# Mixer B: the probabilities turned by VectorE and GpSimd instead of by TensorE

## The chip, the core and the metric

One core of a Trainium2 chip runs the whole program. The metric is the device time of one execution in microseconds (us). An engine works through its own instructions in order: TensorE (PE), VectorE (DVE), ScalarE (ACT), GpSimd (POOL) and SyncE (SP), which issues most of the DMAs. They wait for each other by semaphores.

## What is computed

An encoder of two layers over 256 tokens with 2048 features, all in float32. Layer 0 has mixer A (grouped-query attention), layer 1 has mixer B. A gated MLP follows each mixer. Mixer B is what the change touches. It has 24 heads of 128 features in three groups (windows and dilations (128,1), (512,4), (2048,16)), eight heads to a group:

```python
def dilated_group(q, k, v, rel_bias_g, window, dilation):
    ...                       # keys gathered by stride, masked to the window
    logits = einsum(qb, kb) * scale + bias
    m = max(logits); p = exp(logits - m); l = sum(p)
    o = einsum(p, vb) / l
    return o, m + log(l)      # and the log of the softmax denominator

def mixer_b(h, w_qkv, w_o, rel_bias):
    qkv = h @ w_qkv
    ...                       # outs, log_zs of the three groups
    wts = softmax(stack(log_zs), axis=0)
    y = concat([wts[g] * outs[g] for g in range(3)])
    return y @ w_o
```

The product of probabilities and values needs the probabilities with the keys on the partitions. The softmax leaves them with the queries on the partitions. So each 128x128 block of probabilities has to be turned (transposed) once. This turning is what the change is about.

## The kernel before

The work is a long row of projections. A weight matrix is streamed from HBM in pieces of 4 x 128 rows by 512 columns. `feed` handles one piece: two DMAs of 512 KB into `raw`, and for each half of the piece one "tile" of 128x1024 numbers. ACT rounds the tile to a high part `wh` (L156), VectorE subtracts to get the low part `wl` (L157), and TensorE multiplies it in 12 matmuls of 512 columns (L144, L145, L146: high by high, low by high, high by low). There are four buffers each of `raw`, `wh` and `wl`, so ACT and VectorE can be at most four tiles ahead of TensorE. The subtraction and rounding are given a priority 60 instructions ahead of their place, so that they come early in their engines' order.

All attention work is written as Python generators that are put into a list (`start`). Each half piece of a projection calls `step`, which advances the first generator by one `yield`. So the attention of one projection is interleaved, step by step, with the matmuls of the next ones. The order on every engine is fixed when the program is built.

Mixer B goes over two halves (`hf`) of four heads per group. In each half the keys and queries of the three groups are projected first; `k_gen` and `s_gen` turn them and compute the scores and the exponentials `pr`. The end of the last `s_gen` computes the combined weights `e` from all three groups' maxima and sums (L785 to L793). Then the values of groups 0, 1 and 2 are projected, and for each `v_gen(g, ...)` starts:

- before the change, one step of `v_gen` handles one head: VectorE multiplies `pr` by the weights `e` (L807), TensorE turns the result block by block into PSUM (L809, by a multiplication with the identity), and ACT and VectorE copy it to SBUF as `pT` (group 0: split in a high and a low part, L196 and L197; groups 1 and 2: one copy on ACT or VectorE in turn, L68 or L70). The next step multiplies `pT` and the values (L210 to L212 in group 0, L208 in groups 1 and 2) and splits the product into `ah` and `al`.
- group 0 has 2x2 blocks for a head, groups 1 and 2 have two: 16 + 8 + 8 blocks in a half, 64 in all.

`stg` (two buffers), `qTh`, `qTl`, `kTh`, `kTl` are names of SBUF buffers. In this stretch they have no other use: they hold the scaled projections and the turned queries and keys while `k_gen` and `s_gen` run.

VectorE has a transpose of its own, used elsewhere in the kernel (`block_T`, L237): it turns blocks of 32x32, each within its 32 partitions. To bring a block to another 32 partitions, `block_T` writes 32 partitions at a time, sixteen instructions for a tile.

Of the kernel before, what the change touches and what calls it, by code (L numbers as in the profile page):

```python
# [7 lines left out]
F32 = mybir.dt.float32  # L8
F32R = mybir.dt.float32r
AF = mybir.ActivationFunctionType  # L10
ALU = mybir.AluOpType
AX = mybir.AxisListType

P = 128
D = 2048
NT = 256
# [12 lines left out]
def tile_encoder(ctx: ExitStack, tc: tile.TileContext, x, xT, w_a, w_ao, q_gain, k_gain, w_b, w_bo,  # L29
                 rel_bias, gains, w_up, conv, w_down, final_norm, rope, ident_c, onehot, out):  # L30
    nc = tc.nc
# [10 lines left out]
    ident = cpool.tile([P, P], F32, name="ident")  # L42
# [13 lines left out]
    def nm(s):  # L56
        uid[0] += 1
        return f"{s}_{uid[0]}"

    def ps_tile():  # L60
        return psp.tile([P, 512], F32, tag="ps", name=nm("ps"))
# [3 lines left out]
    def copy(o, i):  # L65
        turn[0] ^= 1
        if turn[0]:
            nc.scalar.activation(o, i, AF.Copy)  # L68
        else:
            nc.vector.tensor_copy(o, i)  # L70
# [121 lines left out]
    def split(hi, lo, src):  # L192
        if lo is None:
            copy(hi, src)
            return
        nc.scalar.activation(hi, src, AF.Copy)  # L196
        nc.vector.tensor_tensor(lo, src, hi.bitcast(F32), ALU.subtract)  # L197
# [7 lines left out]
    def mm3(o, lhsT, rhs, ls, rs, start, stop):  # L205
        (lh, ll), (rh, rl) = lhsT, rhs
        if ll is None:
            nc.tensor.matmul(o, lh[ls], rh[rs], start=start, stop=stop)  # L208
            return
        nc.tensor.matmul(o, lh[ls], rh[rs], start=start, stop=False)  # L210
        nc.tensor.matmul(o, lh[ls], rl[rs], start=False, stop=False)  # L211
        nc.tensor.matmul(o, ll[ls], rh[rs], start=False, stop=stop)  # L212

    def pair_tile(pool, shape, tag, bufs=1, whole=False):
        if whole:
            return pool.tile(shape, F32, tag=tag + "h", name=nm(tag), bufs=bufs), None
        return tuple(pool.tile(shape, F32R, tag=tag + c, name=nm(tag + c), bufs=bufs) for c in "hl")
# [5 lines left out]
    def new_slot(kt):  # L223
        return (hpool.tile([P, NT], F32R, tag=f"ah{kt}", name=nm("ah")),
                hpool.tile([P, NT], F32R, tag=f"al{kt}", name=nm("al")))
# [254 lines left out]
    def evac_split(pool, accs, rstd, whole=False):  # L480
        hi, lo = pair_tile(pool, [P, 2, 512], "v", 1, whole)
        for m in range(2):
            split_scaled(hi[:, m, :], lo if lo is None else lo[:, m, :], accs[m], rstd[:, m:m + 1])
        return hi, lo
# [14 lines left out]
    def heads_T_dve(o, s, pool, tag):  # L499
# [7 lines left out]
        if lo is not None:  # L507
            split(hi, lo, t)

    def mixer_a():  # L510
        with tc.tile_pool(name="apool", bufs=1) as ap:
            junk = junk_of(ap)
# [110 lines left out]
            v = evac_split(ap, va, rstd[0])  # L623
# [85 lines left out]
    def mixer_b(hT, ss_in):  # L709
        with tc.tile_pool(name="bpool", bufs=1) as bp:  # L710
# [25 lines left out]
            allp = slice(None)  # L736
            for hf in range(2):
# [3 lines left out]
                probs = []  # L741
                e = small.tile([P, 3, 8], F32, tag="e", name=nm("e"))
# [49 lines left out]
                    nc.vector.reciprocal(mn, mn)  # L792
                    nc.vector.tensor_tensor(e, e, mn[:, None, :].to_broadcast([P, 3, 8]), ALU.mult)  # L793

                def v_gen(g, accs, hf=hf, probs=probs, e=e):
                    v = evac_split(bp, accs, rstd, g > 0)
                    pTs = {}
                    yield
                    for k in range(5):
                        yield  # L800
                        if k < 4:
                            i = k
                            pr = probs[4 * g + i]
                            t = ps_tile()
                            for m in range(2):
                                c = 4 * m + i
                                nc.vector.tensor_scalar(pr[m], pr[m], e[:, g, c:c + 1], None, op0=ALU.mult)  # L807
                                for kt in range(2 if g == 0 else 1):
                                    nc.tensor.transpose(t[:, kt * NT + m * P:kt * NT + (m + 1) * P],  # L809
                                                        pr[m][:, kt * P:(kt + 1) * P], ident)  # L810
                            pT = pTs[i] = pair_tile(bp, [P, 2 * NT], "pT", 2, g > 0)
                            n = 2 * NT if g == 0 else NT
                            split(pT[0][:, :n], pT[1] if pT[1] is None else pT[1][:, :n], t[:, :n])
                        if k >= 1:
                            i = k - 1
                            j = i % 2
                            pT = pTs.pop(i)
                            if j == 0:
                                o = ps_tile()
                            for kt in range(2):  # L820
                                vs = (allp, kt, slice(i * P, (i + 1) * P))
                                if g == 0:
                                    mm3(o[:, j * NT:(j + 1) * NT], v, pT, vs,
                                        (allp, slice(kt * NT, (kt + 1) * NT)), kt == 0, kt == 1)
                                else:
                                    mm3(o[:, j * NT + kt * P:j * NT + (kt + 1) * P], v, pT, vs,
                                        (allp, slice(kt * P, (kt + 1) * P)), True, True)
                            sl = (2 * g + hf) * 4 + i
                            slots[sl] = new_slot(sl)
                            hi, lo = slots[sl]  # L830
                            split(hi, lo, o[:, j * NT:(j + 1) * NT])

                for g in range(3):
                    bts = biases(hf, g)
# [6 lines left out]
                for g in range(3):  # L841
                    start(v_gen(g, project(w_b, 6 * g + 4 + hf, hT, kgs)))
            return *out_proj(w_bo, slots, [0, 2, 4, 1, 3, 5], 3, 3, junk, bp, "vl"), cw

    hT, ss, cw = mixer_a()
    hT, ss = ffn(0, hT, ss, cw, 2, False, bias_lines)
    hT, ss, cw = mixer_b(hT, ss)
# [85 lines left out]
```

## Time and profile before

| | |
|---|---|
| three runs | 2293.26, 2293.84, 2293.91 us (median 2293.84) |
| profiled execution | 2293.58 us, its span 2291.6 us |
| PE busy | 2279.6 us (99%) |
| DVE busy | 1632.4 us (71%) |
| ACT busy | 1220.7 us (53%) |
| POOL busy | 151.6 us (7%) |

The span runs from the first to the last instruction of the core; some 2 us of the execution lie outside it. Mixer B runs from about 997 to 1555 us of the span. The turning of probabilities (L809) begins at 1160.8 us in the first half and at 1374.3 us in the second.

### The profile page before, as it was taken

Reading aid. Unit: us, or ns where it says so; the run is one execution under the profiler, and the core shown is the slowest. Engines: PE = TensorE matmul, PEld = TensorE weight load, DVE = VectorE, ACT = ScalarE, POOL = GpSimd, SP = SyncE. Lnnn points to the kernel's source line nnn. Section 1 sums busy time; section 2 is a strip of 40 time slices with the busy share of each in tenths; the row PEclk is TensorE's granted clock in tenths of the full one; section 3 lists DMA queues with packets and bytes.
Section 4 is the critical chain, followed back from the end, with each engine's and each line's share of the span. In section 5 each row is a group of like instructions: output and inputs, shape, how many; then the busy total and the mean of one; then the engine's idle time right before and its main releaser. Section 6 shows DMA issues by size and latency. Waiting matters only on the chain.

```text
span 2291.6 us, 31034 instructions
## 1 busy us (share of the span) xinstructions
PE 2279.6 (99%) x11633; PEld 1945.6 (85%) x11633; DVE 1632.4 (71%) x2280; ACT 1220.7 (53%) x1746; POOL 151.6 (7%) x147
## 2 busy tenths in 40 slices
PE   9999999999999999999999999999999999999998
PEld 7888888888888888888888888888888888888886
DVE  6877877775557776878866885677777744777754
ACT  7565565554345554545454554445555533555543
POOL 2331000000000000010000000000000000000010
PEclk9999999999999999999999999999999999999999
DMA  8545655566655556576655554566555566565564
GB/s 300 166 132 162 202 191 187 188 192 190 193 193 189 190 191 191 186 217 208 188 171 181 180 189 164 176 200 204 191 187 190 187 195 194 190 191 187 192 191 149
DMA packets 257015, 433.43 MB, mean 189 GB/s; under 512 B 13784, under 2 KB 194776, under 8 KB 256736
## 3 DMA queue, kind: packets, MB, share of 16 engines
q1 hardware_dynamic: 254912, 425.64, 57.7%
q0 software_dynamic: 1520, 5.25, 1.1%
q8 instruction: 91, 1.49, 0.3%
q10 hardware_dynamic: 432, 0.56, 0.1%
q14 instruction: 60, 0.49, 0.1%
HBM read 429.20 MB, written 2.20 MB: 188 GB/s over the span
## 4 chain that ended last, share of the span: by engine, by line
PE 98%; DVE 1%; issue 1%; DMA 0%; ACT 0%; POOL 0%; SPq 0%; POOLq 0%; DVEq 0%; ACTq 0%
PE acc L123 28%; PE acc L145 17%; PE acc L146 17%; PE acc L144 17%; PE acc L121 15%; PE ps L208 1%; PE ps L211 1%; PE ps L212 0%; PE ps L210 0%; PE ps L665 0%; PE ps L809 0%; DVE wl L157 0%; DVE tT L237 0%; DMA raw<-in_w_a_dram 0%; POOL t L597 0%
## 5 line engine op out<-in xcount | busy, mean ns | idle before, releaser
L157 DVE TENSOR_TENSOR wl<-raw,wh 128x1024 fp32r<-128x1024 f32 (+1 forms) x456 | 553.7, 1217 | 319.6 <-ACT wh L156 316.0
L156 ACT ACTIVATE wh<-raw 128x1024 fp32r<-128x1024 f32 (+1 forms) x456 | 475.4, 1046 | 514.3 <-PE acc L146 443.0
L123 PE MATMUL acc<-xh,wh 128*128 128x512 f32 x2816 | 673.8, 391 | 0.0
L123 PEld LDWEIGHTS acc<-xh,wh 128*128 128x128 f32 x2816 | 517.0, 188 | 100.5 <-DVE v L356 0.4
L112 DVE TENSOR_TENSOR wl<-raw,wh 128x1024 fp32r<-128x1024 f32 x352 | 458.8, 1304 | 194.9 <-ACT wh L111 194.9
L111 ACT ACTIVATE wh<-raw 128x1024 fp32r<-128x1024 f32 x352 | 372.7, 1059 | 208.9 <-issue 77.7
L144 PE MATMUL acc<-wh,ah 128*128 128x512 f32 x1024 | 399.0, 390 | 0.0
L145 PE MATMUL acc<-wl,ah 128*128 128x512 f32 x1024 | 398.5, 389 | 0.0
L146 PE MATMUL acc<-wh,al 128*128 128x512 f32 x1024 | 398.5, 389 | 0.0
L121 PEld LDWEIGHTS acc<-xh,wl 128*128 128x128 f32 x2816 | 361.6, 191 | 14.0
L121 PE MATMUL acc<-xh,wl 128*128 128x256 f32 x2816 | 366.3, 283 | 0.0
L144 PE MATMUL acc<-wh,xh 128*128 128x512 f32 x768 | 302.6, 395 | 1.0 <-ACT wh L156 1.0
L145 PE MATMUL acc<-wl,xh 128*128 128x512 f32 x768 | 299.8, 390 | 0.2 <-DVE wl L157 0.2
L146 PE MATMUL acc<-wh,xh 128*128 128x512 f32 x768 | 299.5, 390 | 0.0
L146 PEld LDWEIGHTS acc<-wh,al 128*128 128x128 f32 x1024 | 192.2, 188 | 39.9
L144 PEld LDWEIGHTS acc<-wh,ah 128*128 128x128 f32 x1024 | 192.3, 188 | 39.6
L145 PEld LDWEIGHTS acc<-wl,ah 128*128 128x128 f32 x1024 | 192.2, 188 | 39.3
L146 PEld LDWEIGHTS acc<-wh,xh 128*128 128x128 f32 x768 | 144.2, 188 | 30.6
L144 PEld LDWEIGHTS acc<-wh,xh 128*128 128x128 f32 x768 | 144.4, 188 | 29.1 <-ACT wh L156 1.4
L145 PEld LDWEIGHTS acc<-wl,xh 128*128 128x128 f32 x768 | 144.4, 188 | 27.8 <-DVE wl L157 0.5
L375 POOL TENSOR_TENSOR cv<-cg,cv 128x512 f32<-128x512 f32 x44 | 62.0, 1408 | 1163.3 <-DVE cv L367 1163.3
L355 ACT ACTIVATE v<-acc 128x256 f32<-128x256 f32 x176 | 66.3, 377 | 113.7 <-PE acc L123 113.7
(156 smaller groups left out, 1364.1 us busy)
## 6 DMA issues: line engine op xcount, KB each, us to landing
raw<-in_w_up_dram SPq DMA_DIRECT2D x352, 512.0 KB, 4.0
raw<-in_w_down_dram SPq DMA_DIRECT2D x176, 512.0 KB, 4.2
raw<-in_w_b_dram SPq DMA_DIRECT2D x144, 512.0 KB, 3.8
raw<-in_w_bo_dram SPq DMA_DIRECT2D x48, 512.0 KB, 3.7
raw<-in_w_a_dram SPq DMA_DIRECT2D x40, 512.0 KB, 4.5
raw<-in_w_ao_dram SPq DMA_DIRECT2D x32, 512.0 KB, 3.7
raw<-in_w_a_dram SPq DMA_DIRECT2D x16, 256.0 KB, 5.8
h<-in_x_dram SPq DMA_DIRECT2D x4, 512.0 KB, 7.6
```

The costliest lines, as they stand in the source:

```text
L111: nc.scalar.activation(wh, rk, AF.Copy)
L112: nc.vector.tensor_tensor(wl, rk, wh.bitcast(F32), ALU.subtract)
L121: nc.tensor.matmul(acc[j][:, :NT], wl[:, kt, c], lhs[4 * kg + kt][0], start=st, stop=sp)
L123: nc.tensor.matmul(acc[j], wh[:, kt, c], lhs[4 * kg + kt][2], start=st, stop=sp)
L144: nc.tensor.matmul(accs[m], xh[:, c], wh[:, j, :], start=st, stop=False)
L145: nc.tensor.matmul(accs[m], xh[:, c], wl[:, j, :], start=False, stop=False)
L146: nc.tensor.matmul(accs[m], xl[:, c], wh[:, j, :], start=False, stop=sp)
L156: nc.scalar.activation(wh[:, c], r[:, c], AF.Copy)
L157: nc.vector.tensor_tensor(wl[:, c], r[:, c], wh[:, c].bitcast(F32), ALU.subtract)
L208: nc.tensor.matmul(o, lh[ls], rh[rs], start=start, stop=stop)
L355: nc.scalar.activation(v[:, j], acc[j][:, NT:], AF.Copy)
L375: nc.gpsimd.tensor_tensor(cv, cg, cv, ALU.mult)
```

## The change

TensorE no longer turns the probabilities. `turn_probs(g)` multiplies them by `e` as before, and VectorE turns each `pr` tile in one instruction over all 128 partitions (`quad_T`): every 32x32 block is turned in place, within its 32 partitions, into a tile `quad` (buffer `stg`, two of them). Then GpSimd moves the blocks to their partitions (`quad_move`): 16 copies of 32 partitions x 256 numbers for each `quad`, into a tile `wide` (buffers `qTh`, `qTl`, `kTh`, `kTl`, one for each of the four quads of a half). Group 0 has two quads in a half (two heads each), groups 1 and 2 one each.

In groups 1 and 2 the matmul reads `wide` directly. In group 0, `wide` is split in a high and a low part as PSUM was before.

The order of the steps changes as well. `v_gen(0)` turns its own two quads first, then that of group 1, and only then begins with its heads; `v_gen(1)` turns the quad of group 2.

```diff
+    def quad_T(quad, at, src):
+        n = src.shape[-1] // P
+        nc.vector.transpose(quad[:, :, at:at + 2 * n - 1:2, :], src.rearrange("p (x c t) -> p c x t", c=4, t=32))
+
+    def quad_move(o, quad):
+        for q in range(4):
+            for c in range(4):
+                nc.gpsimd.tensor_copy(o[32 * c:32 * c + 32, :, 32 * q:32 * q + 32],
+                                      quad[32 * q:32 * q + 32, c])
...
+                def turn_probs(g, probs=probs, e=e, turned=turned):
+                    pairs = 2 if g == 0 else 4
+                    for i0 in range(0, 4, pairs):
+                        if i0:
+                            yield
+                        quad = quad_tile(bp, "stg", 2)
+                        for i in range(i0, i0 + pairs):
+                            for m in range(2):
+                                pr = probs[4 * g + i][m]
+                                nc.vector.tensor_scalar(pr, pr, e[:, g, 4 * m + i:4 * m + i + 1], None,
+                                                        op0=ALU.mult)
+                                quad_T(quad, 8 // pairs * (i - i0) + m, pr)
+                        o = wide_tile(bp, ("qTh", "qTl", "kTh", "kTl")[g + 1 if g else i0 // 2])
+                        quad_move(o, quad)
...
-                def v_gen(g, accs, hf=hf, probs=probs, e=e):
+                def v_gen(g, accs, hf=hf, turned=turned):
                     v = evac_split(bp, accs, rstd, g > 0)
                     pTs = {}
+                    if g == 0:
+                        yield
+                        yield from turn_probs(0)
+                        yield
                     yield
-                    for k in range(5):
+                    if g < 2:
+                        yield from turn_probs(g + 1)
+                    for k in range(1 if g else 0, 5):
                         yield
-                        if k < 4:
-                            i = k
-                            pr = probs[4 * g + i]
-                            t = ps_tile()
-                            for m in range(2):
-                                c = 4 * m + i
-                                nc.vector.tensor_scalar(pr[m], pr[m], e[:, g, c:c + 1], None, op0=ALU.mult)
-                                for kt in range(2 if g == 0 else 1):
-                                    nc.tensor.transpose(t[:, kt * NT + m * P:kt * NT + (m + 1) * P],
-                                                        pr[m][:, kt * P:(kt + 1) * P], ident)
-                            pT = pTs[i] = pair_tile(bp, [P, 2 * NT], "pT", 2, g > 0)
-                            n = 2 * NT if g == 0 else NT
-                            split(pT[0][:, :n], pT[1] if pT[1] is None else pT[1][:, :n], t[:, :n])
+                        if k < 4 and g == 0:
+                            pT = pTs[k] = pair_tile(bp, [P, 2 * NT], "pT", 2)
+                            split(*pT, turned.pop(k))
                         if k >= 1:
                             i = k - 1
...
```

More of the change, by code (lines that the diff above doesn't have):

```diff
@@ L508, in heads_T_dve, with quad_tile, wide_tile @@
             split(hi, lo, t)
+    def quad_tile(pool, tag, bufs=1):
+        return pool.tile([P, 4, 8, 32], F32, tag=tag, name=nm("quad"), bufs=bufs)
+    def wide_tile(pool, tag, bufs=1):
+        return pool.tile([P, 8, P], F32, tag=tag, name=nm("wide"), bufs=bufs)
+    def quad_T(quad, at, src):
[6 more added lines that the diff above has]
+                                      quad[32 * q:32 * q + 32, c])
     def mixer_a():
@@ L793, in s_gen @@
                     nc.vector.tensor_tensor(e, e, mn[:, None, :].to_broadcast([P, 3, 8]), ALU.mult)
-                def v_gen(g, accs, hf=hf, probs=probs, e=e):
+                turned = {}
+                def turn_probs(g, probs=probs, e=e, turned=turned):
[12 more added lines that the diff above has]
+                        quad_move(o, quad)
+                        for i in range(i0, i0 + pairs):
+                            k = 8 // pairs
+                            turned[4 * g + i] = o[:, k * (i - i0):k * (i - i0 + 1)].rearrange("p x c -> p (x c)")
@@ new lines, in attend_v @@
+                def attend_v(g, i, v, o, pT):
+                    j = i % 2
+                    for kt in range(2):
+                        vs = (allp, kt, slice(i * P, (i + 1) * P))
+                        if g == 0:
+                            mm3(o[:, j * NT:(j + 1) * NT], v, pT, vs,
+                                (allp, slice(kt * NT, (kt + 1) * NT)), kt == 0, kt == 1)
+                        else:
+                            nc.tensor.matmul(o[:, j * NT + kt * P:j * NT + (kt + 1) * P], v[0][vs], pT[:, kt * P:(kt + 1) * P],
+                                             start=True, stop=True)
@@ L796, in v_gen @@
+                def v_gen(g, accs, hf=hf, turned=turned):
                     v = evac_split(bp, accs, rstd, g > 0)
                     pTs = {}
+                    if g == 0:
+                        yield
+                        yield from turn_probs(0)
+                        yield
                     yield
-                    for k in range(5):
+                    if g < 2:
+                        yield from turn_probs(g + 1)
+                    for k in range(1 if g else 0, 5):
                         yield
-                        if k < 4:
-                            i = k
-                            pr = probs[4 * g + i]
-                            t = ps_tile()
-                            for m in range(2):
-                                c = 4 * m + i
-                                nc.vector.tensor_scalar(pr[m], pr[m], e[:, g, c:c + 1], None, op0=ALU.mult)
-                                for kt in range(2 if g == 0 else 1):
-                                    nc.tensor.transpose(t[:, kt * NT + m * P:kt * NT + (m + 1) * P],
-                                                        pr[m][:, kt * P:(kt + 1) * P], ident)
-                            pT = pTs[i] = pair_tile(bp, [P, 2 * NT], "pT", 2, g > 0)
-                            n = 2 * NT if g == 0 else NT
-                            split(pT[0][:, :n], pT[1] if pT[1] is None else pT[1][:, :n], t[:, :n])
@@ L814, in v_gen @@
+                        if k < 4 and g == 0:
+                            pT = pTs[k] = pair_tile(bp, [P, 2 * NT], "pT", 2)
+                            split(*pT, turned.pop(k))
                         if k >= 1:
                             i = k - 1
-                            j = i % 2
-                            pT = pTs.pop(i)
-                            if j == 0:
+                            if i % 2 == 0:
                                 o = ps_tile()
[L820 to L827, printed above, removed]
+                            attend_v(g, i, v, o, pTs.pop(i) if g == 0 else turned.pop(4 * g + i))
@@ L830, in v_gen @@
                             hi, lo = slots[sl]
-                            split(hi, lo, o[:, j * NT:(j + 1) * NT])
+                            split(hi, lo, o[:, (i % 2) * NT:(i % 2 + 1) * NT])
                 for g in range(3):
```

## The prediction

> **What bounds the kernel now.** I read the page first, then the chain that ended last within the stretch that changes, then that stretch in order of time, engine by engine.
>
> ```profile
> span 2291.6 us, 31034 instructions
> PE 2279.6 (99%) x11633; PEld 1945.6 (85%) x11633; DVE 1632.4 (71%) x2280; ACT 1220.7 (53%) x1746; POOL 151.6 (7%) x147
> ...
> PE 98%; DVE 1%; issue 1%; DMA 0%; ACT 0%; POOL 0%; SPq 0%; POOLq 0%; DVEq 0%; ACTq 0%
> ...
> by line: PE acc L144 29.7%; PE acc L145 29.7%; PE acc L146 29.5%; PE ps L208 4.5%; PE ps L809 3.7%; PE ps L212 1.0%; PE ps L210 1.0%; PE ps L211 0.9%; PE ps L320 0.3%; issue 0.1%
> ...
> by line: PE acc L144 29.5%; PE acc L145 29.4%; PE acc L146 29.3%; PE ps L208 5.4%; PE ps L809 3.7%; PE ps L211 1.1%; PE ps L212 1.0%; PE ps L210 0.9%; issue 0.1%
> ```
>
> TensorE sets the end: 98% of the chain, and it is never idle for long. The last two lines are the chain in 1150 to 1250 us and in 1350 to 1450 us, the two stretches where probabilities are turned. There too everything on the chain is PE work. So each microsecond taken off PE is won, and each microsecond that PE is made to wait is lost: nothing else has to catch up. A difference under 0.2% (4.6 us) can't be told from none here.
>
> **What goes.** The turning on PE, L809, is 3.7% of each of these stretches of 100 us: 3.7 us in each half, **7.4 us** in all (64 instructions). That is the most the change can win. The four ACT and four VectorE copies out of PSUM of a half (L68, L70) go too. They aren't on the chain.
>
> **What comes to VectorE.** Three rows of its order in time at the turning, then three groups of the page's kind (the number behind the bar is the sum in us, then the mean of one in ns):
>
> ```profile
> 1160.30 1.14 DVE L807 TENSOR_SCALAR pr<-pr,e 128x256 f32<-128x256 f32 x4
> 1161.35 1.22 DVE L157 TENSOR_TENSOR wl<-raw,wh 128x1024 fp32r<-128x1024 f32 x1
> ...
> 1170.00 1.65 DVE L807 TENSOR_SCALAR pr<-pr,e 128x128 f32<-128x128 f32 x8
> ...
> L237 DVE STREAM_TRANSPOSE qT<-stg 32x256 f32<-32x256 f32 x64 | 27.9, 436 | 1.0
> ...
> L197 DVE TENSOR_TENSOR pTl<-ps,pTh 128x512 fp32r<-128x512 f32 x24 | 16.5, 688 | 5.0 <-ACT pTh L196 5.0
> ...
> L197 DVE TENSOR_TENSOR al<-ps,ah 128x256 fp32r<-128x256 f32 x40 | 16.7, 418 | 0.8 <-ACT ah L196 0.2
> ```
>
> A multiplication of 256 columns takes 0.285 us (1.14/4), one of 128 takes 0.21 (1.65/8). A transpose of 256 numbers per partition takes 0.436 over 32 partitions; I take the same over 128, since the partitions work side by side in the other rows. No row has one of 128 numbers. From the L197 rows, 256 numbers more cost 0.27 us, so I estimate 0.436 - 0.135 = 0.30 us, between 0.21 (the cheapest row of that size) and 0.436.
>
> The instruction order of the changed program shows what stands in front of what. VectorE starts at 1160.30, as before. It now runs both quads of group 0 in one piece, 8 x 0.285 + 8 x 0.436 = 5.8 us, up to 1166.1. Then comes one weight subtraction (1.22, to 1167.3). Then, for group 1's quad, 7 multiplications and 6 transposes (1.5 + 1.8) before the next subtraction can start, which ends at 1171.8. In the old order a subtraction stood behind the first four multiplications.
>
> When does PE want that low half? PE's rows in order of time (start, us, line):
>
> ```profile
> 1156.36 0.47 PE L144 MATMUL acc<-wh,xh 128*128 128x512 f32 x1
> ...
> 1159.21 0.39 PE L144 MATMUL acc<-wh,xh 128*128 128x512 f32 x1
> ...
> 1160.34 0.39 PE L146 MATMUL acc<-wh,xh 128*128 128x512 f32 x1
> ...
> 1163.56 0.28 PE L212 MATMUL ps<-pTh,vl 128*128 128x256 f32 x1
> ...
> 1163.68 0.28 PE L210 MATMUL ps<-pTh,vh 128*128 128x256 f32 x1
> ```
>
> Matmuls of 512 columns start 0.226 us apart ((1160.34 - 1159.21)/5), with changes of line in between about 0.229: 2.75 us for a tile of 12. An attention matmul takes 0.12. With L809 gone, four tiles stand between 1159.21 and this one, so PE arrives at 1159.21 + 11.0 + 0.3 = 1170.5. Even without any trouble from GpSimd it waits 1.3 us. Then PE wants the low half of the first head's probabilities, 7 matmuls (1.6 us) later, at 1173.4. On VectorE that is behind a transpose, a multiplication, a subtraction, a transpose and itself: 0.3 + 0.21 + 1.22 + 0.3 + 0.69 = 2.7 us after 1171.8, or 1174.5: 1.1 us more. So PE loses 2.4 us of the 3.7 in each half to VectorE's order alone.
>
> **What comes to GpSimd.** 64 copies of 32 x 256 numbers in a half, 16 for a quad. Before, it has next to nothing to do here. Two groups and two rows in time show what its instructions take elsewhere:
>
> ```profile
> L694 POOL CAST oh<-oc 128x1024 fp32r<-128x1024 f32 x1 | 1.0, 1043 | 4.3 <-DMA oc<-in_onehot_dram 4.3
> ...
> L696 POOL CAST rh<-rb 128x24 fp32r<-128x24 f32 x1 | 0.2, 203 | 0.2 <-DMA rb<-in_rel_bias_dram 0.2
> ...
> 24.79 0.46 POOL L530 TENSOR_TENSOR ct_k<-rp,gbs 128x128 f32<-128x128 f32 x1 [9.19 <-DMA gbs<-in_k_gain_dram]
> 25.21 0.60 POOL L534 TENSOR_TENSOR st_k<-rp,gbs 128x64 f32<-128x64 f32 x2
> ```
>
> No copy of this shape is in the trace. Between 24 numbers (0.203) and 1024 (1.043) the slope is 0.84 ns a number, so 256 numbers take 0.203 + 232 x 0.00084 = 0.40 us. One GpSimd instruction starts 0.04 before the one ahead has ended (24.79 + 0.46 against 25.21). So a copy takes **c = 0.36 us**. The bounds are 0.16 (the 24 numbers, less the overlap) and 1.0 (the 1024). I take 0.36 because 256 lies near the lower row; the strided output speaks for somewhat more.
>
> **What they do to each other.** Both engines in order of time at two places of the MLP, and two groups:
>
> ```profile
> 295.07 1.22 DVE L112 TENSOR_TENSOR wl<-raw,wh 128x1024 fp32r<-128x1024 f32 x1
> ...
> 295.30 2.14 POOL L375 TENSOR_TENSOR cv<-cg,cv 128x512 f32<-128x512 f32 x1 [17.31 <-DVE cv L367]
> ...
> 314.19 1.29 POOL L375 TENSOR_TENSOR cv<-cg,cv 128x512 f32<-128x512 f32 x1 [16.75 <-DVE cv L367]
> ...
> 314.61 1.96 DVE L112 TENSOR_TENSOR wl<-raw,wh 128x1024 fp32r<-128x1024 f32 x1 [0.56 <-ACT wh L111]
> ...
> L427 DVE TENSOR_SCALAR part<-part 128x2 f32<-128x2 f32 x1 | 0.8, 845 | 0.0
> ...
> L272 DVE TENSOR_SCALAR ms<-ssq 128x8 f32<-128x8 f32 x5 | 0.8, 160 | 0.0
> ```
>
> These rows decide the forecast. The subtraction and GpSimd's product don't run side by side. At 295.07 the subtraction was first; the product takes 2.14 in place of 1.29 and ends 1.15 after it. At 314.19 the product was first; the subtraction takes 1.96 in place of 1.22 and ends 1.08 after it. The multiplication by a scalar is held too: L427 took 0.845 on two numbers while GpSimd worked, L272 takes 0.160. So GpSimd's copies and VectorE's subtractions and multiplications take turns, one whole instruction each.
>
> The Trainium skill has this rule in "SBUF — State Buffer", section "Who interferes with whom": the pair of ports that VectorE and GpSimd share goes to whichever starts first, for the whole instruction, and is wanted by VectorE's two-input operations and by its two-port modes. The rows agree. It also says that a VectorE instruction with one SBUF input outside those modes doesn't contend; no row here shows it for a transpose. If transposes were held as well, the sum below would rise by 4 x 0.436 + 16 x 0.30 = 6.5 us in each half, to 2321.
>
> Now the sum. GpSimd starts when the first quad is turned: 1160.30 + 2.9 = 1163.2. PE's first matmul of group 1 reads the third batch of copies. Up to the end of that batch the shared turn is taken by 48 copies (48c) and by VectorE's 4 multiplications of 256 and 16 of 128 (1.1 + 3.4), 6 subtractions (7.3) and 4 of `pTl` (4 x 0.69 = 2.8; their input comes from SBUF now): 14.6 us. So the batch is there at 1163.2 + 48c + 14.6. Unhindered, PE gets there after 8 tiles and 24 attention matmuls: 1159.21 + 22.0 + 2.9 = 1184.1. PE's loss in a half is 48c - 6.3, with c = 0.36 **11.0 us**.
>
> A check in between: the third quad writes into the first one's buffer (`stg` has two), so VectorE has to wait until the first 16 copies are done, at 1163.2 + 5.8 + 4 x 0.285 + 1.22 + 2 x 0.21 = 1171.8. Two subtractions stand behind that wait. The first of them then ends after 1.8 (transposes) + 1.05 (multiplications) + 1.22 and some 1.6 us of turns lost to copies: 1177.5, 7.0 us after PE wants it. ACT waits for the same copies (`pTh`) with the rounding of the next tiles behind it. So most of the 11 us is seen as waits for `wl`, the rest at `pTh`, `pTl` and the first read of `wide`. The fourth batch isn't wanted until two dozen us later and costs PE nothing. On the POOL queue the last bias DMA stands ahead of the first copy; SP's weight loads keep their places.
>
> Net: 2 x (11.0 - 3.7) = +14.6 us on the profiled 2293.6, which is 0.3 under the median of the runs: 2308.2, or **2308.5** against the median. In general the change is 96c - 20 us, zero at c = 0.21.
>
> **The rivals.** (1) *Copies don't hold VectorE*, since they touch 32 partitions only or come in gaps. For it: no row has such a copy. Against it: the four rows above, whole instructions each time. PE then loses 2.4 to VectorE's order, 2 x (2.4 - 3.7) = -2.6 us: 2291. It decides if subtractions stay at 1.22 us beside copies. Not slower, within 0.2%.
> (2) *Copies are dear*, c of 0.5 to 0.7 for the move across partitions and the strided output: +28 to +47, 2322 to 2341. At the upper bound of 1.0 it is +76, 2370. For it: nothing in the trace moves numbers between partitions on GpSimd. Against: the cast rows have the same kind of instruction.
> (3) *All is hidden*: transposes nearer 0.2, turns that fall well, PE loses nothing: -7.4, 2286.4. Against: the wait of 2.4 comes out of VectorE's own rows.
> That the change doesn't do what it says is out: the program's order has no turning of probabilities left on PE in mixer B.
>
> **How the numbers follow.** My forecast (taking turns, c up to 0.5) gets 0.62, rival 2 0.17, rival 1 0.15, rival 3 0.06. Faster by over 0.2% is rival 3 alone: 0.06. Within 0.2%: rival 1 less a little, 0.13. Slower: 0.81, the small remainder of rival 1 with it. The range runs from 2292, just above rival 1's value, to 2328, c = 0.56.
>
> **What would show it.** Right: L157 rows in 1160 to 1200 us of up to 1.5 us instead of 1.22; PE idle of some 11 us in each half, ended by `wl`, `pTl`, `pTh` or `wide`; GpSimd busy almost without a gap for over 30 us from 1163; copies 0.36 apart when alone. Wrong: subtractions at 1.22 throughout, or PE without idle time in that stretch.

## The result, and the profile after

The changed kernel takes 2305.15 us (median; 2304.7 to 2306.88), the kernel before beside it 2293.77: a ratio of 1.005, interval 1.004 to 1.006. It is 11.4 us slower; the forecast was 14.7 slower (2308.5, range 2292 to 2328). The profiled execution took 2305.57 us.

From the page of the changed kernel (its span, the busy times, the chain by engine), then the chain within 1150 to 1250 us by line, then its group of copies (`wide` is the name of the tile that the copies fill):

```profile
span 2303.8 us, 31066 instructions
PE 2277.3 (99%) x11569; PEld 1941.8 (84%) x11569; DVE 1645.2 (71%) x2320; ACT 1217.5 (53%) x1738; POOL 227.3 (10%) x275
...
PE 94%; POOL 3%; DVE 2%; issue 1%; DMA 0%; ACT 0%; SPq 0%; POOLq 0%; DVEq 0%; ACTq 0%
...
by line: POOL wide L523 28.5%; PE acc L145 19.4%; PE acc L146 19.1%; PE acc L144 19.1%; PE ps L839 3.8%; issue 2.6%; DVE quad L518 1.4%; PE ps L208 1.4%; DVE wl L157 1.1%; DVE pr L822 1.1%; DVE lg L785 0.4%; DVE nmx L786 0.4%; ACT e L804 0.
...
L523 POOL COPY wide<-quad 32x256 f32<-32x256 f32 x128 | 75.3, 588 | 189.3 <-DVE quad L518 184.0
```

PE's busy time fell by only 2.3 us, although 7.4 us of turning went. The chain, all PE in this stretch before, now runs through GpSimd's copies for 28.5% of the 100 us. GpSimd is busy 10% of the span: the page's first part alone would never point to it.

What PE waited for in the first half (1150 to 1210 us; in the second the same four waits come to 6.9):

```profile
PE acc L145 <- DVE wl L157: 2.6, 1, 2.6
PE ps L839 <- POOL wide L523: 1.9, 1, 1.9
PE ps L210 <- ACT pTh L196: 1.4, 1, 1.4
PE ps L210 <- DVE al L197: 1.1, 1, 1.1
```

That is 7.0 us. The starts of the same weight matmuls in both traces, one subtracted from the other, give 5.7 us for the first half and 5.6 for the second (the changed kernel's trace is also 1.0 us late from its first 10 us on, which is not the change). With 3.7 us of turning gone, 9.4 us were lost in the first half: the 7.0 of waits, and 2.4 more. PE's rows in order of time say where the 2.4 went, and so do the windows (the stretch and its length, then PE, PEld, DVE, ACT and POOL busy, the granted clock, the DMAs' share and GB/s):

```profile
1170.85 0.39 PE L146 MATMUL acc<-wh,xh 128*128 128x512 f32 x1
1172.61 0.39 PE L210 MATMUL ps<-pTh,vh 128*128 128x256 f32 x1 [1.37 <-ACT pTh L196]
1172.83 0.39 PE L144 MATMUL acc<-wh,xh 128*128 128x512 f32 x1
1175.82 0.50 PE L145 MATMUL acc<-wl,xh 128*128 128x512 f32 x1 [2.60 <-DVE wl L157]
...
1176.55 0.63 PE L144 MATMUL acc<-wh,xh 128*128 128x512 f32 x1
1176.97 0.63 PE L145 MATMUL acc<-wl,xh 128*128 128x512 f32 x1
```
```profile
1160.00:1170.00 10.00, 10.00 (x46) 8.29 (x45) 7.75 (x24) 3.36 (x4) 5.61 (x12) 1.00 0.49 115
1170.00:1180.00 10.00, 6.03 (x22) 4.51 (x21) 8.07 (x19) 3.16 (x5) 9.36 (x16) 0.83 0.31 102
```

Between the matmuls of 1170.85 and 1175.82 PE ran only two. From 1176.55 on, matmuls of 512 columns start 0.42 us apart instead of 0.23, until 1178.7. TensorE's clock had been lowered: the granted clock is 0.50 from 1176.2 to 1179.6. A clock of 0.83 over 10 us is 1.7 us lost. The other 0.7 belong to the four waits themselves: a matmul's row is 0.39 long, but the next one usually starts 0.23 after it, so each wait costs some 0.16 more than its idle time. The Trainium skill ("TensorE: Matmul & The Clock Gate", Part 1) says that the clock falls to half after an idle window of about 3.4 us. The rows agree on the half; but here the two idle times were 1.4 and 2.6 us, with two matmuls between them, so a full idle window of that length wasn't needed. The prediction had no term for the clock.

The last of the four waits decides what the rest is worth. PE reads the third batch at 1194.47, 0.05 us after its last copy has ended, and GpSimd copies without a gap from 1163.93 on. So the 1.7 us of slow clock probably add nothing to the total here: a faster PE would have waited as much longer for that batch (no run of this order keeps the clock up and the batch late).

### The profile page after: what moved, and what is told of

Same layout as the page of the kernel before. It is cut to its first block, busy times and chain, and to the rows that moved or that the text cites. A ratio compares the mean times of both kernels' runs of the same rounds, so it can differ in the third digit from the quotient of the medians.

```text
span 2303.8 us, 31066 instructions
## 1 busy us (share of the span) xinstructions
PE 2277.3 (99%) x11569; PEld 1941.8 (84%) x11569; DVE 1645.2 (71%) x2320; ACT 1217.5 (53%) x1738; POOL 227.3 (10%) x275
## 4 chain that ended last, share of the span: by engine, by line
PE 94%; POOL 3%; DVE 2%; issue 1%; DMA 0%; ACT 0%; SPq 0%; POOLq 0%; DVEq 0%; ACTq 0%
PE acc L123 28%; PE acc L145 16%; PE acc L144 16%; PE acc L146 16%; PE acc L121 15%; POOL wide L523 2%; DMA raw<-in_w_a_dram 0%; DVE wl L157 0%; PE ps L210 0%; PE ps L212 0%; PE ps L211 0%; PE ps L839 0%; PE ps L681 0%; PE ps L208 0%; DVE tT L237 0%
```

## The experiments

Times are medians; each run has the kernel before beside it (2293.6 to 2294.0). Four theories to begin with (more letters come with the expectations). **A**: the many copies on GpSimd come too late. **B**: VectorE's new order is the cost. **D**: it is the one buffer for which VectorE waits. **E**: copies cost time by holding VectorE, whoever needs their result.

**One copy per quad.**

```diff
 def quad_move(o, quad):
-    for q in range(4):
-        for c in range(4):
-            nc.gpsimd.tensor_copy(o[32*c:32*c+32, :, 32*q:32*q+32], quad[32*q:32*q+32, c])
+    nc.gpsimd.tensor_copy(o.rearrange("p x (c t) -> p c x t", c=4), quad)
```

> The changed kernel, with one GpSimd copy of 128 x 1024 numbers in place of the 16 copies of 32 x 256 of each quad: the blocks are left in their own partitions (the movement between partition quadrants is left out), and everything on VectorE, ScalarE and TensorE is as in the changed kernel. Theory A (the cost is the many copies on GpSimd, one third of a microsecond each and more where a weight subtraction stands between them): a copy takes 1.1 to 1.5 us, the third batch is there long before TensorE wants it, and what is left is the loss to VectorE's order, 2.4 us in each half, against 3.7 won: 2290 to 2294. Rival B (the cost is on VectorE itself: the turning in its queue ahead of the weight subtractions): the time stays within 2 us of the changed kernel, 2303 to 2307, with the waits for wl and pTh as they were.

This kernel leaves out the movement between partitions. Measured: 2293.74 us (ratio 1.000, 0.999 to 1.0009). The 11.4 us go with the 64 copies of a half: A. That it is their number and not the crossing to other partitions, the changed kernel's trace shows: of the 16 copies of a quad, the four that stay in their partitions take 0.39 to 0.40 us where nothing holds them, as the twelve others do. What is left is one wait in each half, and VectorE's and GpSimd's rows ahead of it:

```profile
PE ps L211 <- DVE pTl L197: 2.6, 1, 2.6
```
```profile
1172.97 1.95 POOL L521 COPY wide<-quad 128x1024 f32<-128x1024 f32 x1 [4.28 <-DVE quad L518]
1173.95 1.52 DVE L197 TENSOR_TENSOR pTl<-wide,pTh 128x512 fp32r<-128x512 f32 x1
```

The prediction had worked out 2.4 us for VectorE's order alone. But 0.8 of the 2.6 are the one big copy: `pTl` takes 1.52 us beside it, and 0.69 without (L197 in the prediction). That leaves about 1.8 for VectorE's order. The total is still 2.7 us above what the prediction made of that order (2291). In the first half the clock fell again after this gap (0.85 in 1170 to 1180), in the second it did not. The weight matmuls' starts, against the kernel before, lose 0.5 us over the first half and gain 1.2 over the second: with the same wait in both, the difference of 1.7 is the slow clock. So B holds as well, as a smaller part.

**Half of the copies on ScalarE** (the result is kept):

```diff
+    if (q + c) % 2:
+        nc.scalar.activation(dst, blk, AF.Copy)
+    else:
         nc.gpsimd.tensor_copy(dst, blk)
```

> The changed kernel with every second one of the 16 copies of a quad on ScalarE (activation Copy), the others on GpSimd: the same result. Theory A (GpSimd's chain of copies sets the arrival of the third batch): 24 copies less stand in front of the third batch, at 0.44 us each 10.6 us; it is there before TensorE wants it, the waits for wide go, VectorE's wait for its third quad's buffer shrinks from 3.8 us to under 1, and 2.4 us of VectorE's order are left: 2291 to 2296. Rival C (ScalarE has no room either: 8 copies of some 0.35 us in a burst ahead of the rounding of the next weight tile): the wait for wl goes and one for wh of the same size takes its place, 2300 to 2306.

Measured: 2294.1 us (0.9992 to 1.0011), as A had it. The waits in the first half:

```profile
PE ps L210 <- ACT pTh L196: 1.5, 1, 1.5
PE ps L210 <- DVE al L197: 1.2, 1, 1.2
PE ps L842 <- DVE al L197: 0.9, 1, 0.9
```

Waits for `wl` and `wide` are gone, no wait is for `wh`, and the clock stays at 1.00 in this stretch. What remains, 3.6 us, just eats the 3.7 won.

**A buffer of its own for the third quad.**

```diff
-quad = quad_tile(bp, "stg", 2)
+quad = quad_tile(bp, "kTl") if g == 1 else quad_tile(bp, "stg", 2)
```

> The changed kernel with a buffer of its own for the third quad (group 1), so that VectorE need not wait until GpSimd has emptied the first one: the wait of 3.8 us in each half goes. Theory A (the third batch of copies comes too late by GpSimd's own chain, whoever waits first): the wait for wl of 2.6 us in a half shrinks to 1 or less and the wait for wide grows by about as much; without the gap of almost 5 us around it TensorE's clock keeps 1.0 and 2 us a half come back: 2299 to 2304. Rival D (that buffer is the cause: it alone holds up the subtractions): the waits for wl and pTh and the slow clock go, wide stays at 1.9, 2293 to 2297.

Measured: 2306.46 us (1.0041 to 1.0071), no gain:

```profile
PE ps L210 <- ACT pTh L196: 3.7, 1, 3.7
PE ps L839 <- POOL wide L523: 1.9, 1, 1.9
PE ps L210 <- DVE al L197: 1.0, 1, 1.0
PE ps L211 <- DVE pTl L197: 0.4, 1, 0.4
```

D falls: VectorE no longer waits for the buffer, and PE waits as long as before, 7.0 us, now for `pTh`, which reads the same batches. A's number was 2.5 us too low: a gap of 4 us stayed and with it the slow clock (0.83).

**Copies that nobody reads**, in the kernel before:

```diff
+def idle_copies(tag, e=e):
+    iw = bp.tile([P, 8, P], F32, tag=tag, name=nm("iw"))
+    nc.vector.tensor_copy(iw[:, 0, ::32], e[:, 0, :4])
+    ...                # 16 gpsimd.tensor_copy, 32x256, from bt0 into iw
 for k in range(5):
+    if g == 0 and k < 3 or g == 1 and k == 0:
+        idle_copies(...)
```

> The kernel before (TensorE turns the probabilities), and 64 GpSimd copies of the same shape in each half at the same places, from a table that was loaded earlier into tiles that nobody reads; four tiny VectorE writes set when each batch may start. Only the copies' presence is added. Theory A (the copies cost time because others wait for their results, not because they hold VectorE now and then): weight subtractions take 1.4 us and more in place of 1.2 beside them, the weight tiles are made some 8 us ahead of TensorE's need, and the time stays within 1.5 us of the kernel before, 2293 to 2295. Rival E (holding VectorE is enough): TensorE waits for wl, 2297 to 2303.

Measured: 2297.7 us (1.0008 to 1.0027), 3.8 us slower. This is E's time, but not E's way: no wait of PE for `wl` shows. PE's waits in the first half, then the multiplications of the whole run (shortest, median, longest in ns), here and in the kernel before:

```profile
PE ps L210 <- DVE al L197: 1.0, 1, 1.0
PE ps L211 <- DVE pTl L197: 0.3, 1, 0.3
```
```profile
L818 DVE TENSOR_SCALAR pr<-pr,e x48: 273/355/515, 1160.5 to 1389.6; 128x128 f32<-128x128 f32 x32, 128x256 f32<-128x256 f32 x16
```
```profile
L807 DVE TENSOR_SCALAR pr<-pr,e x48: 278/284/353, 1160.3 to 1384.9; 128x128 f32<-128x128 f32 x32, 128x256 f32<-128x256 f32 x16
```

The copies hold up VectorE, and PE sees it in the short chains of attention and not in the weight subtractions, which have slack. The eight tiny VectorE writes that gate the copies are part of these 3.8 us.

**The turning spread out.** VectorE turns one head in a step, group 1's and 2's turning stands between the attention steps of the group before, and group 1's values get a buffer of their own:

```diff
 def turn_probs(g, ...):
         for i in range(i0, i0 + pairs):
+            if i:
+                yield
 def v_gen(g, accs, ...):
+    t = turn_probs(g + 1) if g < 2 else iter(())
     for k in range(1 if g else 0, 5):
         yield
         ...            # split, attention of one head
+        next(t, None)
```

It was run in three forms: with half of the copies on ScalarE, with all on GpSimd (and five more steps of delay), and with one copy per quad (the movement between partitions left out).

> The changed kernel with both causes taken away, the result kept: one head is turned in each step between weight tiles (no burst on VectorE), the turning of groups 1 and 2 stands between the attention steps of the group before, every second copy is on ScalarE, and group 1's values have a buffer of their own so that its rounding need not wait for group 0's attention. Theory A (loss = VectorE's burst + the late batches, both gone): no wait over 1 us in the turning, 5 to 7 us of the 7.4 are kept, 2287 to 2290. Rival F (beside GpSimd's copies the short chains through VectorE, multiplication, low half, attention output, come late whatever the order, about 2 us in each half as in the run with copies that nobody reads): 2290 to 2293. Rival C (ScalarE's copies delay its rounding): waits for wh or pTh, 2293 or more.

> As the spread version, but all 64 copies of a half on GpSimd, with two more steps ahead of the first split and three more ahead of group 1's attention, so that each batch of 16 has about four steps (11 us) to land. GpSimd needs 16 x 0.44 = 7.0 us and the turns that subtractions take, some 3 us: just enough. Theory A: nobody waits long for wide, 2288 to 2292. Rival F (holding VectorE costs about 2 us in each half whatever the order): 2291 to 2294. If a batch still lands late: waits for wide or pTh of 1 to 3 us a half, 2293 to 2300.

> The spread order with one GpSimd copy of 128 x 1024 numbers for each quad (blocks not moved between partitions: the movement is left out). Against the changed kernel with the same single copy in the old order (2293.7) it takes away VectorE's burst alone. Theory A (the burst costs 2.4 us and the slow clock behind it some 1 us in each half): 2286 to 2288.5. Rival (TensorE waits there for something else, the transposes themselves or ScalarE): 2291 to 2294.

Measured: 2293.83 (0.9991 to 1.001), 2304.52 (1.0031 to 1.0061), 2289.94 (0.9973 to 0.9992). All three are above theory A's ranges. The third lies between the two that were expected, and the second is outside everything expected, with one wait of 7.1 us in each half. In all three, the waits are ended by `al`. In the first form (PE's waits of the first half; then, in order of time, the rows of ACT, DVE and PE around the longer one):

```profile
PE ps L210 <- DVE al L197: 2.1, 1, 2.1
PE ps L842 <- DVE al L197: 0.9, 1, 0.9
```
```profile
1173.09 2.96 ACT L156 ACTIVATE wh<-raw 128x1024 fp32r<-128x1024 f32 x3
1175.95 0.36 ACT L196 ACTIVATE ah<-ps 128x256 fp32r<-128x256 f32 x1
...
1177.27 1.18 DVE L157 TENSOR_TENSOR wl<-raw,wh 128x1024 fp32r<-128x1024 f32 x1
1178.38 0.41 DVE L197 TENSOR_TENSOR al<-ps,ah 128x256 fp32r<-128x256 f32 x1
...
1178.84 0.39 PE L210 MATMUL ps<-pTh,vh 128*128 128x256 f32 x1 [2.06 <-DVE al L197]
```

Why should attention wait for `al`, which only the output projection reads? Because two heads share a PSUM tile, and in this program PE does not write the second head's half before VectorE has read the first's. So the chain from PE to ACT, to VectorE and back to PE has to close within one step of 2.75 us. ACT came to `ah` after three roundings, VectorE to `al` after a subtraction.

**A PSUM tile for each head**, in four of the kernels above:

```diff
-if i % 2 == 0:
-    o = ps_tile()
+o = ps_tile()
```

> The spread version with half of the copies on ScalarE, and with a PSUM tile for each head's attention output in place of one for two heads. Theory G (what TensorE still waits for there is not the batches but the PSUM tile: the second head's first matmul waits until VectorE has made the first head's low half, al, from the same tile, and that subtraction stands behind turning and weight subtractions): the waits of 2.1 and 0.9 us in each half go, no other over 0.5 us takes their place, 2287 to 2289. Rival H (al is only the last of several that come late; pTl or wh is next): 2290 to 2293.

> The spread order with one copy of a whole quad (the movement between partitions is left out), and with a PSUM tile for each head. Nothing is left that TensorE should wait for, so that this is the most that the change can win: theory G 2286.0 to 2287.5 (the 7.4 us of turning, less waits under 0.3 us). Rival H: 2288 to 2290.

> The changed kernel's order with every second copy on ScalarE, and with a PSUM tile for each head. The run without the last edit had 3.6 us of waits in a half: pTh 1.5, al 1.2 and 0.9. Theory G: the two for al go, pTh stays, 2289 to 2291. Rival H: another wait takes the place of al, 2292 to 2294.

> The kernel before with the copies that nobody reads, and with a PSUM tile for each head. Its run without the last edit lost 2.0 us in each half, half of it waiting for al. Theory G (copies that hold VectorE's multiplications cost time only through that tile): the wait for al of 1.0 and 1.2 us goes, 2294.5 to 2296, some of the small waits for pr and pTl stay. Rival (VectorE is late everywhere, so the next thing waits instead): 2297 to 2298.

Measured: **2286.01** us (0.9955 to 0.9979), 2285.59 (0.9951 to 0.9978), 2290.55 (0.9977 to 0.9995), 2296.89 (1.0004 to 1.0023). The first, the spread version with half of the copies on ScalarE, keeps the result and beats both kernels. It comes out even below its range, and the view of waits lists none for PE in either half's turning. Its windows, in the same columns as before:

```profile
1160.00:1170.00 10.00, 10.00 (x46) 8.27 (x45) 9.90 (x23) 7.81 (x14) 6.33 (x10) 1.00 0.61 172
1170.00:1180.00 10.00, 10.00 (x51) 8.50 (x50) 8.97 (x24) 9.63 (x18) 3.69 (x7) 1.00 0.51 159
1180.00:1190.00 10.00, 10.00 (x54) 8.52 (x52) 8.82 (x23) 8.55 (x18) 8.56 (x13) 1.00 0.47 156
```

In the old order the tile takes the two waits for `al` away and leaves the one for `pTh` (1.5 us). With the copies that nobody reads it takes `al` away too, but the time falls by only 0.8 us: 0.9 us of waits for `pTl` came in its place. That lies between the two expectations: VectorE is late at more than one place.

**The same with all copies on GpSimd**, and with the five more steps of delay for them:

> The spread version with all copies on GpSimd and a PSUM tile for each head's attention output: against the best version it lacks only ScalarE's share of the copies, and has more steps of delay for them. Theory J (GpSimd's chain is still too long: the turning of group 2 stands ahead of the third head's low half pTl on VectorE and waits for a buffer that GpSimd has yet to empty): the wait for al of 7.1 us in each half becomes one for pTl or pTh of 3 to 5 us, 2292 to 2298. Rival G (only the shared PSUM tile mattered): no wait over 1 us, 2286 to 2289.

Measured: 2298.9 us (1.0013 to 1.0032), a little above theory J's range, with its wait. PE's wait of the first half, then the rows of ACT and VectorE in which they wait for GpSimd, and VectorE's `pTl` that ends PE's wait:

```profile
PE ps L211 <- DVE pTl L197: 4.2, 1, 4.2
```
```profile
1173.04 1.16 ACT L196 ACTIVATE pTh<-wide 128x512 fp32r<-128x512 f32 x2 [6.59 <-POOL wide L523]
1173.70 0.73 DVE L197 TENSOR_TENSOR pTl<-wide,pTh 128x512 fp32r<-128x512 f32 x1 [3.83 <-ACT pTh L196]
...
1184.53 0.51 DVE L518 STREAM_TRANSPOSE quad<-pr 128x128 f32<-128x128 f32 x2 [0.74 <-POOL wide L523]
...
1189.75 0.68 DVE L197 TENSOR_TENSOR pTl<-wide,pTh 128x512 fp32r<-128x512 f32 x1
```

The buffer that theory J named holds VectorE up for 0.74 us only. Most of the delay comes earlier: the first batch keeps ACT, and through `pTh` VectorE, waiting for 3.83 us, and VectorE then has hardly a free moment until the `pTl` of 1189.75. In the best version VectorE waits for no batch in this half, and ACT 0.4 us. So ScalarE's share of the copies is worth most of these 13 us. Not all of them can be put down to it: the steps of delay differ too, and the clock fell in both halves (0.50 for 3.4 us each, so 3.4 of the 13).

## Why the prediction was right, step by step

**PE bounds, and the turning is worth 7.4 us: right.** When nothing is late, the time falls by 7.9 us (ratio 0.9967, interval 0.9955 to 0.9979), by 8.3 with one copy per quad. The interval is 4.8 to 10.3 us, so the 7.4 lie within it.

**VectorE's order costs 2.4 us a half: near in size, not in place.** The run with one copy per quad has one wait of 2.6, some 1.8 without the copy that holds `pTl`. All of it is at `pTl`; the 1.3 us that were to be spent on `wl` don't show. Spreading the turning lowers that run by 3.8 us (2293.74 to 2289.94), the slow clock of its first half included. The price of 2291 in rival 1 left out that clock.

VectorE's rows in order of time, GpSimd's run of copies of a half, and the groups of copies and of subtractions beside them (1160 to 1200; shortest, median, longest in ns), the last one in the kernel before:

```profile
1161.29 0.61 DVE L822 TENSOR_SCALAR pr<-pr,e 128x256 f32<-128x256 f32 x2
1161.82 0.77 DVE L518 STREAM_TRANSPOSE quad<-pr 128x256 f32<-128x256 f32 x2
...
1163.68 0.78 DVE L822 TENSOR_SCALAR pr<-pr,e 128x256 f32<-128x256 f32 x2
1164.39 0.76 DVE L518 STREAM_TRANSPOSE quad<-pr 128x256 f32<-128x256 f32 x2
...
1171.93 0.51 DVE L518 STREAM_TRANSPOSE quad<-pr 128x128 f32<-128x128 f32 x2 [3.80 <-POOL wide L523]
...
1174.36 1.41 DVE L157 TENSOR_TENSOR wl<-raw,wh 128x1024 fp32r<-128x1024 f32 x1
```
```profile
1163.93 40.33 POOL L523 COPY wide<-quad 32x256 f32<-32x256 f32 x64 [5.16 <-DVE quad L518]
```
```profile
L523 POOL COPY wide<-quad x128: 387/398/1486, 1163.9 to 1423.0; 32x256 f32<-32x256 f32 x128
```
```profile
L157 DVE TENSOR_TENSOR wl<-raw,wh x10: 1177/1314/1414, 1166.4 to 1199.1; 128x1024 fp32r<-128x1024 f32 x10
```
```profile
L157 DVE TENSOR_TENSOR wl<-raw,wh x12: 1219/1226/1227, 1161.4 to 1197.2; 128x1024 fp32r<-128x1024 f32 x12
```

**A copy takes 0.36 us: too low.** Its duration, 0.398, is the 0.40 of the cast rows. But the next starts 0.44 after it: a gap of 0.04 where I had taken an overlap of 0.04. The 48 copies up to the third batch are 21.1 us and not 17.3.

**14.6 us of turns with VectorE: too high.** The third batch ends at 1194.42 by the trace, 30.5 us after the first copy; without 21.1 that leaves 9.4. A copy that meets a weight subtraction takes some 1.3 us, and the next one starts about 1.34 after it. So each such subtraction takes 0.9 of GpSimd's time, about what the four rows of the MLP had. Eight of them fall into this stretch, 7.2 us, where the sum had six at 1.22, 7.3: that term came out by luck. The low halves `pTl` and `al` make most of the rest. The multiplications hardly count: two of them go from 0.61 to 0.78 us beside copies, and 33 of the 47 distances between copies stay at 0.43 to 0.48, although multiplications run there. So the 4.5 us for them are the term that failed. They rested on one row (L427, 0.845), where the multiplication was the one that waited. Transposes aren't held at all (0.77 and 0.76), as the Trainium skill has it ("SBUF — State Buffer", "Who interferes with whom"); the same section counts such multiplications among those that can take the shared ports, which the copies here hardly felt.

**PE loses 11.0 us a half: 9.4.** The two errors, +3.8 and -5.2, partly cancel, and that is luck: with the copy at 0.44 alone put right the forecast would have been +22, with the turns alone +4. PE reads the third batch at 1194.47; unhindered it would be there at 1184.1, or 1185.1 with the 1.0 us by which this trace is late.

**Where the 11 us would be seen: wrong.** "Most as waits for `wl`" is 2.6 of 7.0. VectorE's wait for `stg` ends at 1171.93, near what was worked out (1171.8, or 1172.8 in this later trace), but the subtraction after it ends at 1175.8 and not at 1177.5 (1178.5). Of the 1.6 us of turns that it was to lose, its own row of 1.41 shows 0.2. And 1.7 us are no waits at all, but the lowered clock.

**Net: +14.6 forecast, +11.4 measured.** The mechanism, GpSimd's copies in turns with VectorE, holds: taking the copies away, or moving half of them to ScalarE, brings the time back to 2293.7 and 2294.1. The wrong sign that I named, subtractions at 1.22 us beside copies, didn't show: they go up to 1.41. In its sum the prediction priced the copies only through those who wait for their results; 3.8 us for copies that nobody reads show that there is a second way.

## What to carry to other kernels

An engine that is idle 93% of the time can still be too slow for a burst: add up the burst against the moment at which its last result is read, and count what it shares with its neighbours. When work leaves the bounding engine, look at what the old order relied on: here two heads in one PSUM tile were harmless until VectorE and ScalarE became busy, and in the spread version a tile for each was worth 7.8 us. The whole gain needed three things together: without the PSUM tile 2293.8, without the spreading 2290.6, without ScalarE's share of the copies 2298.9 (with some steps of delay more).

## What the runs showed of the hardware

- A gap of TensorE can cost more than its length. After idle times of 1.4 and 2.6 us with two matmuls between (the changed kernel), and after single ones of 3.7 and 4.2 us, the granted clock was 0.50 for 3.4 us and matmuls of 512 columns started 0.43 us apart. After one of 7.1 us it was 0.50 for 6.8 us, the last 2.3 of the idle time among them. After one of 2.6 us it happened in one half and not in the other. After 2.1 us and less it did not happen in the profiled executions. But the run with waits of 2.1 us lists a clock of 0.997 or 0.998 in eight of its ten executions and 0.999 in the profiled one, so there it probably happened in others.
- A copy of 32 x 256 numbers to other partitions takes 0.398 us on GpSimd and 0.416 on ScalarE. Beside VectorE's subtractions GpSimd's mean is 0.588 (the changed kernel); ScalarE's longest is 0.420, in the run with half of them there.
- GpSimd's copies lengthen VectorE's multiplications with a scalar (from 0.283 to 0.346 us for 128 columns and from 0.349 to 0.411 for 256, means of the run with copies that nobody reads), though these lengthen the copies little.
